# Queries and forget gates of six HGRN heads as seven block products, with their weight sums formed in the SSD

## The chip, the core and the metric

One core of a Trainium2 chip runs the whole kernel. The metric is the device time of one execution in microseconds (us), as the median of several runs. The engines are named as in the profile: PE is TensorE, DVE VectorE, ACT ScalarE, POOL GpSimdE and SP SyncE.

## The reference

The model has two layers over 512 tokens of width 1024, in float32. Layer 0 mixes the tokens by a Mamba-2 SSD, layer 1 by an HGRN2; after each mixer come a layer norm, an MLP with squared ReLU, another layer norm and a gated embedding. What matters here is the start of the HGRN: one projection to 4 x 1024 columns, of which the first two quarters are the queries `q` and the raw forget gates `fz`, split into 8 heads of 128 columns.

```python
q, f, v, g = split(u @ w_in, 4)         # u: 512 x 1024, w_in: 1024 x 4096; f is fz
log_f = logaddexp(log(lb), log1p(-lb) + log_sigmoid(fz))
k = (1 - lb) * sigmoid(-fz)
# per head, chunks of 64 tokens: a gated linear recurrence over q, k, v with decay f,
# then o = rms_norm(o) * silu(g), and o @ w_out
```

## The kernel before

**Products.** Each float32 operand is split into a high part `hi` (rounded to the fast float32 format fp32r) and the rest `lo`, and a product takes three matmuls, hi·hi, hi·lo and lo·hi: `mm3`, lines L120 to L122. For a weight, `unit` loads a tile of 128 x 1024 through SP's queue into a `raw` buffer, ScalarE casts it to `whi` (L114), and VectorE subtracts to get `wlo` (L116).

**Queries and gates.** `qf(h)` makes q and f of head h. Each is one PSUM bank `pj` of 128 x 512 (head columns by tokens): 8 steps over the model width, each an `mm3` with a 128 x 128 weight and 512 columns of tokens, so 24 matmuls for q and 24 for f. ScalarE copies q out of its bank (L1173), and makes f and k from the other one: two sigmoids (L1177, L1180) and two scalings (L1178, L1181). There are four `pj` banks in all.

**Block products.** `gated(i)`, which makes v and g of four heads at a time, uses a scheme with seven block products instead of eight (a Strassen-like one): the activations' sums `s1` to `s4` are formed in the HGRN's lead-in, and the weights' sums in the SSD, by `sums_early`, which loads four quarters on POOL's queue into one tile `b8`, adds and subtracts on VectorE (L437 and following), and stores the sums to device memory (`pre_h`), from where the HGRN reads them as ordinary weights. One PSUM bank there collects several products, and is read between them.

**Order of work.** TensorE's instructions run in the order in which the code writes them. On the other engines a scheduler puts them in order by its own estimate of when each can run. In the HGRN TensorE's work comes from two generators that are interleaved by hand. The foreground is `scores(n)` and `tail(n)` for pair n of heads: score matmuls (`blocks`, L1263 and L1371), which VectorE masks and multiplies into place (L1294, L1295, L1306, L1275), and a tail of transposes, value products (L1432, L1434), the norm (ScalarE's squares L1438 and square root L1441, VectorE's reciprocal L1443 and scaling L1447). The background is the list `JOBS`: `q0` to `q7` are the heads' `qf`, `b0` and `b1` the two `gated`, `o` the output projection. Between steps of the foreground `fill(amount)` takes background work worth that amount (a full-width `mm3` counts 0.68); the amounts are in `GAPS`, a row for each pair of heads.

In the SSD a loop over k = 1 to 8 makes two steps a round, and calls `next(sums)` up to three times in round 1 and twice in the others.

Of the kernel before, what the change touches and what calls it, by code (L numbers as in the profile page):

```python
# [32 lines left out]
SUMS = (60, 300, 300, 300)  # L33

JOBS = "q0 s0 q1 s1 q2 q3 b0 q4 q5 q6 q7 b1 o".split()
LEADIN = 6.0
GAPS = (6.0, 12.0, 10.0, 10.0), (13.0, 9.5, 9.5, 9.5), (10.0, 10.0, 10.0, 10.0), (14.0, 5.0, 4.0, 3.5), (3.0, 2.0, 2.5, 0.0)
CONSTS = dict(ident=P, triu=P, eps=1, convw=96, convb=24, dskip=16, snw=16, dtc=2, hlb=8, hnw=1)


# [1 line left out]
def trunk(ctx: ExitStack, tc, a):  # L42
# [21 lines left out]
    def mk(p, shape, tag, dt=F32, **kw):  # L64
        return p.tile(list(shape), dt, tag=tag, name=nm(tag), **kw)
# [34 lines left out]
    def behind(ins):  # L100
        return nullcontext() if ins is None else tc.issue_after(ins.ins)
# [323 lines left out]
    def sums_early(w, dst):  # L425

        for u in range(2):
            for h in range(2):
                cs = slice(h * 512, (h + 1) * 512)
                t = mk(b8, [P, 4, T], "b8")  # L430
                nc.gpsimd.tensor_copy(t[:, :, 0], toks[0][:, :, 0])
                w00, w01, w10, w11 = (t[:, i] for i in range(4))
                for x, src in zip((w01, w11, w00, w10), (w[0][1], w[1][1], w[0][0], w[1][0])):
                    nc.gpsimd.dma_start(x, src[u][:, cs])
                yield
                with behind(marks["pe"]):
                    nc.vector.tensor_sub(w11, w11, w01)  # L437
# [556 lines left out]

    whvg = a["whvg"]
    heads = [[[[whvg[8 * i + 4 * n + 2 * r + u] for u in range(2)] for n in range(2)] for r in range(2)] for i in range(2)]
    sums = (step for i in range(2) for step in sums_early(heads[i], a["pre_h"][i]))

    PIECES = {3: (0, 4), 4: (2, 2), 5: (0, 4), 6: (2, 2)}

    with tc.manual_schedule(engines={mybir.EngineType.PE}):
        bcm[0] = bc_group(0)
        for j in range(2):
            load_decay(j)
            x_part(j)
            z_part(j)
        prep[0] = bc_prep(bcm[0], bank(pst, "pt"), bank(psy, "py0"))
        toks.extend(dt_tail())
        turn_pair(0, (bank(psy, "py1"), bank(psj, "pj")))
        for k in range(1, 9):  # L1010
            i, j = 2 * k, 2 * k + 1
            mine, theirs = PIECES.get(k, (0, 0))
            with behind(conv[1][1] if k == 1 else None):
                decays(i - 2)
            if k < 8:
                if k in (4, 6):
                    bcm[k // 2] = bc_group(k // 2)
# [144 lines left out]
    def qf(h):  # L1162
# [18 lines left out]
        nc.scalar.activation(kk, kk, AF.Copy, scale=lbc[:, h : h + 1])  # L1181
# [22 lines left out]
    def background():  # L1204
        first = gated(0)
        for _ in range(8):
            yield next(first)
        for f in late:
            f()
        for job in JOBS:  # L1210
            i = int(job[1:] or 0)
            if job == "o":
                yield from out0()
            elif job[0] == "s":
                nc.gpsimd.dma_start(a["xd"][:, i], acc[:, i])
# [392 lines left out]
```

## Time and profile before

| | |
|---|---|
| median of 3 runs | 1392.22 us (1392.14 to 1393.08) |
| the profiled execution | 1393.39 us |
| its span (first to last instruction) | 1391.6 us |
| TensorE busy | 1385.1 us (100%) |
| VectorE / ScalarE / GpSimdE busy | 79% / 58% / 4% |
| SSD, about | 0 to 330 us |
| HGRN, about | 755 to 990 us |

All times inside the span are counted from its start. A row of the timeline gives start, duration, engine, line, operation, destination and sources, shape and count, and in brackets how long the engine stood idle before it and what released it. A row of a line's view gives the duration's minimum, median and maximum in ns. A row of a stretch gives, behind its length, the busy time and instruction count of PE, its weight loads, DVE, ACT and POOL, then the clock granted to TensorE, the share of the DMA engines and GB/s. `mean ns of one` for a matmul counts overlapped time; the pitch of its starts is what it costs.

### The profile page before, as it was taken

To read this page: it belongs to the slowest core of one execution; us is meant where nothing else is said; L and a number is where in the kernel's file an instruction comes from. 1 tells how busy PE (TensorE), PEld (TensorE's weight loads), DVE (VectorE), ACT (ScalarE), POOL (GpSimd) and SP (SyncE) were. 2 spreads that over 40 slices of the span, in tenths; PEclk is the share of its full clock that TensorE was granted. 3 is DMA by queue.
4 is the path that set the end of the run, shared out by engine and by line. 5 is a ranking of instruction groups with operands and counts; after the bars stand their busy time and mean duration, and the time that the engine had idled before them with its cause. 6 is when DMAs were issued, how large, how long until landed. Compare 5 with 4: busy or idle time off the path is not lost.

```text
span 1391.6 us, 20632 instructions
## 1 busy us (share of the span) xinstructions
PE 1385.1 (100%) x7885; PEld 1157.9 (83%) x7885; DVE 1104.6 (79%) x1734; ACT 811.7 (58%) x1309; POOL 50.4 (4%) x101
## 2 busy tenths in 40 slices
PE   9999999999999999999999999999999999999998
PEld 7888888888988888888888888888888888888887
DVE  7798976686867879778889886878785887769886
ACT  7877667485455455546466465674555554545563
POOL 0220200100000000000000000000000000000000
PEclk9999999999999999999999999999999999999999
DMA  8675533523354665654385343254263656646374
GB/s 290 220 254 171 212 137 130 188 97 101 114 206 151 213 221 171 209 186 165 106 305 195 124 145 99 93 178 143 97 221 128 205 185 216 219 151 210 107 247 148
DMA packets 74819, 241.96 MB, mean 174 GB/s; under 512 B 9056, under 2 KB 9696, under 8 KB 74592
## 3 DMA queue, kind: packets, MB, share of 16 engines
q1 hardware_dynamic: 57792, 197.64, 42.2%
q0 software_dynamic: 7712, 26.22, 5.3%
q10 hardware_dynamic: 9216, 16.78, 3.3%
q8 instruction: 62, 1.02, 0.3%
q14 instruction: 37, 0.30, 0.1%
HBM read 211.18 MB, written 29.43 MB: 173 GB/s over the span
## 4 chain that ended last, share of the span: by engine, by line
PE 92%; DVE 3%; ACT 2%; DMA 2%; issue 0%; POOL 0%; SPq 0%; DVEq 0%; ACTq 0%
PE pj L120 23%; PE pj L122 23%; PE pj L121 23%; PE py L120 5%; PE py L122 5%; PE py L121 5%; DMA raw<-in_wssd 1%; PE py L939 1%; PE py L1263 1%; DVE cv L811 1%; DVE wlo L116 1%; ACT b L906 1%; PE py L941 1%; DMA acc<-in_xw 0%; PE pt L922 0%
## 5 line engine op out<-in xcount | busy, mean ns | idle before, releaser
L114 ACT CAST whi<-raw 128x1024 fp32r<-128x1024 f32 x234 | 244.8, 1050 | 256.5 <-PE pj L121 125.0
L116 DVE TENSOR_TENSOR wlo<-raw,whi 128x1024 fp32r<-128x1024 f32 x234 | 284.8, 1222 | 131.3 <-ACT whi L114 129.9
L120 PE MATMUL pj<-b,whi 128*128 128x512 f32 (+1 forms) x992 | 377.9, 382 | 0.0
L121 PE MATMUL pj<-b,whi 128*128 128x512 f32 (+1 forms) x992 | 375.8, 379 | 0.0
L122 PE MATMUL pj<-b,wlo 128*128 128x512 f32 (+1 forms) x992 | 375.8, 379 | 0.0
L122 PEld LDWEIGHTS pj<-b,wlo 128*128 128x128 f32 x992 | 186.5, 188 | 35.1
L121 PEld LDWEIGHTS pj<-b,whi 128*128 128x128 f32 x992 | 186.6, 188 | 34.6
L120 PEld LDWEIGHTS pj<-b,whi 128*128 128x128 f32 x992 | 186.1, 188 | 34.8
L122 PE MATMUL pj<-whi,b 128*128 128x512 f32 (+1 forms) x482 | 187.5, 389 | 0.0
L120 PE MATMUL pj<-whi,b 128*128 128x512 f32 x448 | 176.7, 395 | 0.0
L121 PE MATMUL pj<-wlo,b 128*128 128x512 f32 x448 | 174.4, 390 | 0.0
L114 ACT CAST whi<-r 128x1024 fp32r<-128x1024 f32 x64 | 67.2, 1053 | 89.6 <-PE pj L121 67.7
L122 PEld LDWEIGHTS pj<-whi,b 128*128 128x128 f32 x482 | 90.5, 188 | 18.8 <-DVE b L1458 0.2
L120 PE MATMUL py<-whi,b 128*128 128x512 f32 x256 | 100.4, 392 | 0.0
L122 PE MATMUL py<-whi,b 128*128 128x512 f32 x256 | 99.7, 389 | 0.0
L121 PE MATMUL py<-wlo,b 128*128 128x512 f32 x256 | 99.6, 389 | 0.0
L116 DVE TENSOR_TENSOR wlo<-r,whi 128x1024 fp32r<-128x1024 f32 x64 | 77.8, 1220 | 27.4 <-ACT whi L114 26.8
L120 PEld LDWEIGHTS pj<-whi,b 128*128 128x128 f32 x448 | 84.1, 188 | 17.4 <-ACT b L1457 0.3
L121 PEld LDWEIGHTS pj<-wlo,b 128*128 128x128 f32 x448 | 84.2, 188 | 16.9
L120 PEld LDWEIGHTS py<-whi,b 128*128 128x128 f32 x256 | 48.1, 188 | 10.2 <-DVE acc L489 0.5
L122 PEld LDWEIGHTS py<-whi,b 128*128 128x128 f32 x256 | 48.0, 188 | 10.1
L121 PEld LDWEIGHTS py<-wlo,b 128*128 128x128 f32 x256 | 48.1, 188 | 9.8
(421 smaller groups left out, 2083.8 us busy)
## 6 DMA issues: line engine op xcount, KB each, us to landing
raw<-in_w SPq DMA_DIRECT2D x112, 512.0 KB, 3.8
r<-in_w SPq DMA_DIRECT2D x64, 512.0 KB, 4.0
raw<-in_wssd SPq DMA_DIRECT2D x38, 512.0 KB, 4.7
a<-csd SPq DMA_DIRECT2D x16, 512.0 KB, 4.1
b<-in_whvg POOLq DMA_DIRECT2D x32, 256.0 KB, 5.4
pre_h<-b POOLq DMA_DIRECT2D x32, 256.0 KB, 3.0
raw<-in_wso SPq DMA_DIRECT2D x16, 512.0 KB, 4.1
pre<-sg ACTq DMA_DIRECT2D x32, 256.0 KB, 4.7
```

Of the source, the lines that this page charges most:

```text
L114: nc.scalar.copy(hi[:, :n], f)
L116: nc.vector.tensor_sub(lo[:, :n], f, f32(hi[:, :n]))
L120: nc.tensor.matmul(out, sh, mh, start=start, stop=False, **kw)
L121: nc.tensor.matmul(out, sh, ml, start=False, stop=False, **kw)
L122: marks["pe"] = nc.tensor.matmul(out, sl, mh, start=False, stop=stop, **kw)
L811: got = nc.vector.scalar_tensor_tensor(cv[:, d:], ps[:, : T - d], convw[:, i, k : k + 1], cv[:, d:], ALU.mult, ALU.add)
L906: nc.scalar.activation(m[:, r, sl], csb[:, r, sl], AF.Relu, scale=-1.0, bias=cs_tok[:, c, 2 * j + r : 2 * j + r + 1])
L939: nc.tensor.matmul(yd[64 * r : 64 * r + 64, sl], xdt[:, c, r, :], m[:, r, sl], start=True, stop=c == 0)
L941: nc.tensor.matmul(yd[64 * r : 64 * r + 64, sl], pv[:, c - 1, r, :], ecs[:, r, (c - 1) * P : c * P], start=False, stop=True,)
L1263: nc.tensor.matmul(ps[r][32 * b : 32 * b + 32, base + n * c : base + n * c + n], kk[r][:, ts], moving(r, 4 * c + b), start=True, stop=True,)
```

## The change

For heads 2 to 7 `qf` is replaced by `qf_blocks`. The four blocks of the product are q and f by two halves of the tokens, and the model width is split in two as well; seven products of 128 x 256, each of four `mm3` steps, take the place of eight. Two banks `px` and `py` hold them: x collects four products one after the other and is read after each; y holds two, z (the other half of `py`) one. The parts that were copied or added out lie in half of a tile `pre`. ScalarE copies after P1, P2 and P3 (L1226, L1229, L1231), VectorE adds after P4, P5 and P6 (L1234, L1236, L1238); after P7 the gates are made (L1241 to L1251), the sigmoids in two halves each. `sums_head` forms the weights' sums, one tile of four loads, four operations and four stores a head. A tile of `sums_early` is now finished in one step instead of two; the first step of round 1 falls away. `GAPS` of pair 3 gets smaller amounts.

```diff
+BLOCKED = (2, 3, 4, 5, 6, 7)
+SUM_STEPS = (1, 1)
-GAPS = ..., (14.0, 5.0, 4.0, 3.5), (3.0, 2.0, 2.5, 0.0)
+GAPS = ..., (9.5, 5.0, 3.7, 3.4), (3.0, 2.0, 2.5, 0.0)
...
                     for n, x in ((2, w11), (0, w01)):
                         nc.gpsimd.dma_start(dst[n, u][:, cs], x)
-                yield
-                with behind(marks["pe"]):
                     nc.vector.tensor_add(w00, w11, w00)
                     nc.vector.tensor_sub(w10, w10, w00)
...
+    def sums_head(w, dst):
+
+        t = mk(b8, [P, 4, T], "b8")
+        nc.gpsimd.tensor_copy(t[:, :, 0], toks[0][:, :, 0])
+        b11, b12, b21, b22 = (t[:, i] for i in range(4))
+        for x, src in zip((b12, b22, b11, b21), (w[1][:, :T], w[1][:, T:], w[0][:, :T], w[0][:, T:])):
+            nc.gpsimd.dma_start(x, src)
+        yield
+        with behind(marks["pe"]):
+            nc.vector.tensor_sub(b22, b22, b12)
+            nc.vector.tensor_sub(b12, b12, b11)
+            ...
+            nc.vector.tensor_add(b11, b22, b11)
+            nc.vector.tensor_sub(b21, b21, b11)
+            ...
-    sums = (step for i in range(2) for step in sums_early(heads[i], a["pre_h"][i]))
+    wholes = [sums_early(heads[i], a["pre_h"][i]) for i in range(2)]
+    wholes[1:1] = [sums_head([a["whq"][2 * h + w] for w in range(2)], a["pre_q"][h]) for h in BLOCKED]
+    sums = (step for whole in wholes for step in whole)
...
             states(k - 1)
-            if k == 1:
-                next(sums)
             decays(i - 1)
...
-            next(sums)
+            if (k, 0) >= SUM_STEPS:
+                next(sums, None)
...
-            next(sums, None)
+            if (k, 1) >= SUM_STEPS:
+                next(sums, None)
...
+    def qf_blocks(h):
+        ...
+        px, py = bank(psj, "pj"), bank(psj, "pj")
+        x, y, z = px[:, 0:256], py[:, 0:256], py[:, 256:512]
+        ...
+        def product(w, at, moving, ps, start):
+            hi, lo = w
+            for k in range(4):
+                c = slice((4 * at + k) * P, (4 * at + k + 1) * P)
+                mm3(ps, hi[:, c], lo[:, c], moving[0](k), moving[1](k), start and k == 0, k == 3, skip_group_check=True)
+                yield 0.36
+        ...
+        raw = unit(a["whq"][2 * h])
+        yield from product(raw, 0, part(0, 0), x, True)
+        nc.scalar.copy(q1, x)
+        t32 = unit(a["pre_q"][h][0])
+        yield from product(t32, 0, block(mix["s3"]), y, True)
+        nc.scalar.copy(fz, y)
+        yield from product(t32, 1, block(mix["s2"]), x, False)
+        nc.scalar.copy(q2, x)
+        t41 = unit(a["pre_q"][h][1])
+        yield from product(t41, 0, part(1, 1), y, False)
+        vec.tensor_add(q2, y, q2)
+        yield from product(t41, 1, block(mix["s1"]), x, False)
+        vec.tensor_add(fz, x, fz)
+        yield from product(raw, 1, part(1, 0), z, True)
+        vec.tensor_add(q1, z, q1)
+        yield from product(unit(a["whq"][2 * h + 1][:, T:]), 0, block(mix["s4"]), x, False)
+        ...
+        nc.scalar.activation(f[:, 0:256], x, AF.Sigmoid)
+        nc.scalar.activation(f[:, 256:512], fz, AF.Sigmoid)
+        ...
-                yield from qf(i)
+                yield from (qf_blocks if i in BLOCKED else qf)(i)
```

The new lines push the numbers of all later ones: `mm3` is L122 to L124, the cast L116, the subtraction L118, and what was L1263 to L1456 in `scores` and `tail` is 70 higher.

What moves where, at three places. First ScalarE while head 2's products run. Ahead of these rows stand the sigmoids of head 1 (`f_6759` and `f_6843` are its f; `qt` is a tile of `scores` for the first pair). Before:

```order
L1180 ACTIVATE k_6762<-pj_6734 128x512
L1178 ACTIVATE f_6759<-f_6759,lb_6566,lbc_6568 128x512 [waits Activation_49]
L1181 ACTIVATE k_6762<-k_6762,lbc_6568 128x512 [waits Activation_49]
L1317 COPY qt_6972<-qo_6862 128x32x4 [waits DVE_49]
L114 CAST whi_7143<-raw_7141 128x1024 [waits DMAHW3_49,PE_49]
L1173 COPY qx_6812<-pj_6777 128x32x16 [waits PE_49]
L114 CAST whi_7149<-raw_7147 128x1024 [waits DMAHW4_49,PE_49]
L1177 ACTIVATE f_6915<-pj_6820 128x512 [waits DVE_49,PE_49]
```

The same place in the changed kernel, where `b_1141_6855` is the tile `pre`, and `pj_6856` and `pj_6857` are `px` and `py` of head 2:

```order
L1200 ACTIVATE k_6846<-pj_6818 128x512
L1198 ACTIVATE f_6843<-f_6843,lb_6650,lbc_6652 128x512 [waits Activation_49]
L1201 ACTIVATE k_6846<-k_6846,lbc_6652 128x512 [waits Activation_49]
L1226 COPY b_1141_6855<-pj_6856 128x256 [waits PE_49]
L1229 COPY b_1141_6855<-pj_6857 128x256 [waits PE_49]
L1387 COPY qt_7133<-qo_6979 128x32x4 [waits DVE_49]
L116 CAST whi_7177<-raw_7175 128x1024 [waits DMAHW3_49,PE_49]
L1231 COPY b_1141_6855<-pj_6856 128x256 [waits PE_49]
L116 CAST whi_7222<-raw_7220 128x512 [waits DMAHW4_49,PE_49]
```

The copies of P1, P2 and P3 (L1226, L1229, L1231) stand in this queue behind head 1's last gates; the third one also stands behind the `qt` copy and a cast.

Second VectorE during head 2, where the score matmuls of the first pair's first step come (`py_1148` and `py_1149` are their banks before, `py_1157` and `py_1158` now). Before:

```order
L116 TENSOR_TENSOR wlo_7145<-raw_7141,whi_7143 128x1024 [waits DMAHW3_49,PE_49,Activation_49]
L1294 TENSOR_TENSOR k_6691<-k_6691,gg_6869 128x128x2 [waits PE_49]
L1295 TENSOR_TENSOR k_6691<-k_6691,f_6688 128x128
L1306 TENSOR_TENSOR scd_6783<-py_1148_6827,mf_6550 128x8x4x4
L1325 TENSOR_TENSOR gg_6976<-tot_6863 128x32 [waits DVE_49]
L1294 TENSOR_TENSOR k_6762<-k_6762,gg_6879 128x128x2 [waits PE_49]
L1295 TENSOR_TENSOR k_6762<-k_6762,f_6759 128x128
L1275 COPY_PREDICATED scd_6783<-mu_6552,py_1148_6827 128x8x3x4 [waits DVE_49]
L1306 TENSOR_TENSOR scd_6784<-py_1149_6828,mf_6550 128x8x4x4
L1275 COPY_PREDICATED scd_6783<-mu_6552,py_1148_6827 128x8x2x4 [waits DVE_49]
L1275 COPY_PREDICATED scd_6784<-mu_6552,py_1149_6828 128x8x3x4 [waits DVE_49]
L1275 COPY_PREDICATED scd_6783<-mu_6552,py_1148_6827 128x32 [waits DVE_49]
```

In the changed kernel:

```order
L1365 TENSOR_TENSOR k_6775<-k_6775,f_6772 128x128
L1376 TENSOR_TENSOR scd_6869<-py_1157_6944,mf_6634 128x8x4x4
L1395 TENSOR_TENSOR gg_7137<-tot_6980 128x32 [waits DVE_49]
L1364 TENSOR_TENSOR k_6846<-k_6846,gg_6996 128x128x2 [waits PE_49]
L1365 TENSOR_TENSOR k_6846<-k_6846,f_6843 128x128
L1345 COPY_PREDICATED scd_6869<-mu_6636,py_1157_6944 128x8x3x4 [waits DVE_49]
L1376 TENSOR_TENSOR scd_6870<-py_1158_6945,mf_6634 128x8x4x4
L1345 COPY_PREDICATED scd_6869<-mu_6636,py_1157_6944 128x8x2x4 [waits DVE_49]
L1345 COPY_PREDICATED scd_6870<-mu_6636,py_1158_6945 128x8x3x4 [waits DVE_49]
L1345 COPY_PREDICATED scd_6869<-mu_6636,py_1157_6944 128x32 [waits DVE_49]
L1345 COPY_PREDICATED scd_6870<-mu_6636,py_1158_6945 128x8x2x4 [waits DVE_49]
L1236 TENSOR_TENSOR b_1141_6855<-pj_6856,b_1141_6855 128x256 [waits PE_49]
```

The addition of P5 (L1236) stands at the end of the score instructions, of which L1364, L1376 and L1345 were L1294, L1306 and L1275.

Third VectorE during head 5, around the output block of the first pair's tail. In the kernel before, at the tail of the second pair, the same instructions with what followed them there:

```order
L1349 TENSOR_TENSOR xc_8350<-qt_8166,tot_8015 128x4x2x32 [waits DVE_49]
L1353 COPY_PREDICATED scd_7950<-mu_6552,py_1321_8131 128x4x16
L1350 TENSOR_TENSOR xc_8350<-xc_8350,tot_8015 128x4x32 [waits DVE_49]
L1443 RECIPROCAL hri_8307<-hms_8297 128x8 [waits Activation_49]
L1353 COPY_PREDICATED scd_7951<-mu_6552,py_1322_8132 128x4x16
L1447 SCALAR_TENSOR_TENSOR qo_8281<-pt_8279,hri_8307,b_6575 128x128 [waits DVE_49]
L1447 SCALAR_TENSOR_TENSOR qo_8281<-pt_8279,hri_8307,b_6575 128x128 x3
L1447 SCALAR_TENSOR_TENSOR qo_8282<-pm_8280,hri_8307,b_6575 128x128 x4
L116 TENSOR_TENSOR wlo_8540<-raw_8536,whi_8538 128x1024 [waits DMAHW5_49,Activation_49]
```

In the changed kernel, where `pj_7909` and `pj_7908` are head 5's `py` and `px`:

```order
L1423 COPY_PREDICATED scd_7550<-mu_6636,py_1269_7784 128x4x16
L1420 TENSOR_TENSOR xc_8031<-xc_8031,tot_7615 128x4x32 [waits DVE_49]
L1513 RECIPROCAL hri_7988<-hms_7978 128x8 [waits Activation_49]
L1423 COPY_PREDICATED scd_7551<-mu_6636,py_1270_7785 128x4x16
L1517 SCALAR_TENSOR_TENSOR qo_7962<-pt_7960,hri_7988,b_6658 128x128 [waits DVE_49]
L1517 SCALAR_TENSOR_TENSOR qo_7962<-pt_7960,hri_7988,b_6658 128x128 x3
L1517 SCALAR_TENSOR_TENSOR qo_7963<-pm_7961,hri_7988,b_6658 128x128 x4
L1234 TENSOR_TENSOR b_1141_6855<-pj_7909,b_1141_6855 128x256 [waits PE_49]
L1236 TENSOR_TENSOR b_1141_6855<-pj_7908,b_1141_6855 128x256 [waits PE_49]
L118 TENSOR_TENSOR wlo_8298<-raw_8294,whi_8296 128x512 [waits DMAHW4_49,Activation_49]
L1238 TENSOR_TENSOR b_1141_6855<-pj_7909,b_1141_6855 128x256 [waits PE_49]
```

The additions of P4 and P5 (L1234, L1236) stand behind the reciprocal and the eight scalings (L1517); on TensorE, the matmuls of that output block stand between P3 and P4.

More of the change, by code (lines that the diff above doesn't have):

```diff
@@ L35 @@
 JOBS = "q0 s0 q1 s1 q2 q3 b0 q4 q5 q6 q7 b1 o".split()
+BLOCKED = (2, 3, 4, 5, 6, 7)
+SUM_STEPS = (1, 1)
 LEADIN = 6.0
-GAPS = (6.0, 12.0, 10.0, 10.0), (13.0, 9.5, 9.5, 9.5), (10.0, 10.0, 10.0, 10.0), (14.0, 5.0, 4.0, 3.5), (3.0, 2.0, 2.5, 0.0)
+GAPS = (6.0, 12.0, 10.0, 10.0), (13.0, 9.5, 9.5, 9.5), (10.0, 10.0, 10.0, 10.0), (9.5, 5.0, 3.7, 3.4), (3.0, 2.0, 2.5, 0.0)
 CONSTS = dict(ident=P, triu=P, eps=1, convw=96, convb=24, dskip=16, snw=16, dtc=2, hlb=8, hnw=1)
@@ L446, in sums_early @@
                         nc.gpsimd.dma_start(dst[n, u][:, cs], x)
+    def sums_head(w, dst):
[8 more added lines that the diff above has]
+            nc.vector.tensor_sub(b12, b12, b11)
+            for to, x in ((dst[0][:, :T], b22), (dst[1][:, T:], b12)):
+                nc.gpsimd.dma_start(to, x)
+            nc.vector.tensor_add(b11, b22, b11)
+            nc.vector.tensor_sub(b21, b21, b11)
+            for to, x in ((dst[0][:, T:], b11), (dst[1][:, :T], b21)):
+                nc.gpsimd.dma_start(to, x)
     def ready(dst, n):
@@ L1182, in qf @@
         made["q", h] = q, f, kk
+    def qf_blocks(h):
+        if "pre" not in mix:
+            mix["pre"] = mk(b8, [P, 2, D], "b8")
+        px, py = bank(psj, "pj"), bank(psj, "pj")
+        x, y, z = px[:, 0:256], py[:, 0:256], py[:, 256:512]
+        part = lambda r, n: tuple(
+            lambda k, f=f: f(4 * r + k, slice(256 * n, 256 * n + 256)) for f in (x_s.h, x_s.l)
+        )
+        block = lambda t: tuple(lambda k, u=u: t[:, u, k, :] for u in range(2))
+        def product(w, at, moving, ps, start):
[4 more added lines that the diff above has]
+                yield 0.36
+        qs = mix["pre"][:, h % 2, 0:512]
+        q1, q2, fz = (mix["pre"][:, h % 2, 256 * n : 256 * n + 256] for n in range(3))
+        raw = unit(a["whq"][2 * h])
[14 more added lines that the diff above has]
+        yield from product(unit(a["whq"][2 * h + 1][:, T:]), 0, block(mix["s4"]), x, False)
+        q = tmp("qx", [P, 32, 40])
+        nc.scalar.copy(
+            q[:, :, 0:16].rearrange("p n (r j) -> p n r j", r=4), qs.rearrange("p (n j r) -> p n r j", n=32, r=4)
+        )
+        f = tmp("f", [P, T])
+        nc.scalar.activation(f[:, 0:256], x, AF.Sigmoid)
+        nc.scalar.activation(f[:, 256:512], fz, AF.Sigmoid)
+        nc.scalar.activation(f, f, AF.Identity, scale=lbc[:, h : h + 1], bias=lb[:, h : h + 1])
+        kk = tmp("k", [P, T])
+        nc.scalar.activation(kk[:, 0:256], x, AF.Sigmoid, scale=-1.0)
+        nc.scalar.activation(kk[:, 256:512], fz, AF.Sigmoid, scale=-1.0)
+        nc.scalar.activation(kk, kk, AF.Copy, scale=lbc[:, h : h + 1])
+        made["q", h] = q, f, kk
@@ L1600 @@
     args["pre_h"] = nc.dram_tensor("pre_h", (2, 4, 2, P, D), F32).ap()
+    args["pre_q"] = nc.dram_tensor("pre_q", (8, 2, P, D), F32).ap()
     args["xd"] = nc.dram_tensor("xd", (P, NCH, D), F32).ap()
```

## The prediction

> **What bounds the kernel now.** I read the head of the page first: how busy each engine is, the granted clock, and the chain of work that ended last.
>
> ```profile
> span 1391.6 us, 20632 instructions
> PE 1385.1 (100%) x7885; PEld 1157.9 (83%) x7885; DVE 1104.6 (79%) x1734; ACT 811.7 (58%) x1309; POOL 50.4 (4%) x101
> PEclk9999999999999999999999999999999999999999
> PE 92%; DVE 3%; ACT 2%; DMA 2%; issue 0%; POOL 0%; SPq 0%; DVEq 0%; ACTq 0%
> ```
>
> TensorE is busy all the time, at its full clock, and carries 92% of the chain. Next I asked what TensorE waits for; these three rows are the whole answer of the view of waits.
>
> ```profile
> PE pm L155 <- DVE y L152: 1.1, 1, 1.1
> PE py L120 <- ACT whi L174: 0.7, 1, 0.7
> PE py L972 <- DVE ss L967: 0.5, 1, 0.5
> ```
>
> 2.3 us in all, none of it in the HGRN. So the time is the length of TensorE's stream of instructions, and a change can act in two ways only: it shortens that stream, or it opens a hole in it. Third, the timeline of TensorE, for the pitch (start to start) of the two shapes in question, since the durations of pipelined matmuls overlap.
>
> ```profile
> 344.79 0.39 PE L121 MATMUL pj<-wlo,b 128*128 128x512 f32 x1
> ...
> 357.26 0.40 PE L122 MATMUL pj<-whi,b 128*128 128x512 f32 x1
> ...
> 367.47 0.28 PE L120 MATMUL pj<-b,whi 128*128 128x256 f32 x1
> ...
> 370.22 0.28 PE L122 MATMUL pj<-b,wlo 128*128 128x256 f32 x1
> ```
>
> 55 intervals lie between the first two rows: 12.47 / 55 = 0.2267 us for 512 columns. 23 lie between the last two: 2.75 / 23 = 0.1196 us for 256. Half the columns cost 53%.
>
> **Part 1: the matmuls.** A head's q and f were 2 x 8 steps of three matmuls, 48 x 0.2267 = 10.88 us. They become 7 products of 12 matmuls, 84 x 0.1196 = 10.05 us. That is 0.83 us a head, and for heads 2 to 7 a gain of 4.98 us, all on the bound.
>
> A reason against this would be the weight loads, of which there are now 84 instead of 48 a head:
>
> ```profile
> L122 PEld LDWEIGHTS pj<-b,wlo 128*128 128x128 f32 x992 | 186.5, 188 | 35.1
> ```
>
> The 256-column row above has a load for each matmul, and its pitch (0.120) is shorter than one load (0.188): the loads overlap and the pitch already holds them. The Trainium skill says otherwise ("TensorE: Matmul & The Clock Gate", The mechanism and LDWEIGHTS): a load of 128 columns takes 107 ns and overlaps with matmuls only where the row groups differ. By it a 256-column matmul would take about 0.107 + 0.107 = 0.213 us and a 512-column one 0.320, a head 17.9 us instead of 15.4, and the six heads would lose some 15 us; the trace disagrees at both shapes (0.120 and 0.227).
>
> **Part 2: work added beside TensorE.** Unit prices:
>
> ```profile
> L114 ACT CAST whi<-raw x234: 1030/1053/1082, 14.8 to 1369.8; 128x1024 fp32r<-128x1024 f32 x117
> L116 DVE TENSOR_TENSOR wlo<-raw,whi x234: 1192/1222/1364, 15.8 to 1371.1; 128x1024 fp32r<-128x1024 f32 x117
> L1139 ACT ACTIVATE b<-pj x8: 375/383/400, 833.7 to 940.5; 128x256 f32<-128x256 f32 x8
> L1132 DVE TENSOR_TENSOR b<-pj,b x8: 407/413/438, 819.9 to 929.3; 128x256 f32<-128x256 f32 x8
> L437 DVE TENSOR_TENSOR b<-b x8: 681/692/694, 50.8 to 253.5; 128x512 f32<-128x512 f32 x8
> ```
>
> In the HGRN a head casts 3.5 weight tiles instead of 2, copies three products out on ScalarE and adds three on VectorE. ScalarE: 1.5 x 1.05 + 3 x 0.38 + about 0.4 for gates cut in halves = 3.1 us. VectorE: 1.5 x 1.22 + 3 x 0.41 = 3.1 us. Six heads: 18.5 us on each. The loads on SyncE's queue grow from 1.0 to 1.75 MB a head. In the SSD, each head adds one tile of sums: 4 loads and 4 stores on GpSimdE's queue, 4 x 0.69 us on VectorE, 16.6 us for six. The room for this:
>
> ```profile
> 55.00:110.00 55.00, 55.00 (x341) 46.38 (x340) 53.49 (x79) 46.41 (x81) 12.29 (x22) 1.00 0.70 235
> 790.00:838.00 48.00, 48.00 (x469) 39.22 (x468) 40.93 (x120) 30.40 (x57) 0.00 (x0) 1.00 0.40 133
> 890.00:941.00 51.00, 51.00 (x506) 42.96 (x505) 39.12 (x103) 34.58 (x80) 2.38 (x5) 1.00 0.47 156
> ```
>
> The columns after TensorE and its loads are VectorE, ScalarE, GpSimdE, clock, DMA share, GB/s. The HGRN has some 15 to 23% of VectorE free, a third of ScalarE, half of the DMA. 18.5 us spread over the 200 us from 780 bring VectorE from about 80 to about 90%: it fits as an average, so as throughput I cost it at nothing. In the SSD the tight place is 55 to 110 us, with VectorE 1.5 us from full. But the heads' sums come in only after the first four whole tiles, as the order of `wholes` in the code has it, at and past that stretch; as many sums as before stand in it. I take 0 there, with 0 to 2.5 us as bounds (four 0.69 us sums falling into it would be 2.8, less a little of the 1.5). Nothing is under zero: no step of the SSD on TensorE got shorter.
>
> **Part 3: the turnarounds, where I put the cost.** A product of 12 matmuls lasts 12 x 0.1196 = 1.44 us, and the seven products P1 to P7 share two PSUM banks in turn. So P3 waits for ScalarE's copy of P1, P4 for that of P2, P5 for that of P3, P6 for VectorE's addition of P4, P7 for that of P5. In the head before, a bank was filled for 5.4 us and four banks went round. Now each copy or addition has one product, 1.44 us, and needs about 0.4 of it; engines work in order, so it is late as soon as more than 1.0 us of other work stands ahead of it. What stands ahead is in the orders shown above; how long it takes is in the trace. Head 2 in rows of before (ScalarE, then TensorE and VectorE):
>
> ```profile
> 780.43 1.05 ACT L114 CAST whi<-raw 128x1024 fp32r<-128x1024 f32 x1 [3.42 <-PE pj L121]
> 781.88 0.59 ACT L1180 ACTIVATE k<-pj 128x512 f32<-128x512 f32 x1
> 783.06 0.72 ACT L1181 ACTIVATE k<-k,lbc 128x512 f32<-128x512 f32 x1
> 786.12 0.30 ACT L1317 COPY qt<-qo 128x128 f32<-128x128 f32 x1 [2.34 <-DVE qo L1288]
> 786.32 1.05 ACT L114 CAST whi<-raw 128x1024 fp32r<-128x1024 f32 x1
> ```
>
> ```profile
> 780.46 0.39 PE L120 MATMUL pj<-b,whi 128*128 128x512 f32 x1
> ...
> 787.35 1.31 PE L1263 MATMUL py<-qx,k 128*32 128x80 f32 x64
> 788.59 0.50 PE L120 MATMUL pj<-b,whi 128*128 128x512 f32 x1
> ```
>
> ```profile
> 788.46 1.22 DVE L116 TENSOR_TENSOR wlo<-raw,whi 128x1024 fp32r<-128x1024 f32 x1
> 789.60 0.42 DVE L1294 TENSOR_TENSOR k<-k,gg 128x256 f32<-128x256 f32 x1
> ...
> 792.88 0.34 DVE L1326 TENSOR_TENSOR gg<-tot,gg 128x32 f32<-128x32 f32 x1
> ```
>
> - P1 runs 780.46 to 781.90. P2 needs a bank that the k sigmoid of head 1 frees at 781.88 + 0.59 = 782.47: stall 0.57.
> - P2 ends 783.91. The copy of P1 stands behind head 1's last gate, 783.06 + 0.72 = 783.78, and ends 784.16: P3 stalls 0.25.
> - P3 ends 785.60, P4 787.04. The copy of P3 stands behind the qt copy, which VectorE's L1288 holds until 786.12, and the cast behind it: 787.37 + 0.38 = 787.75. P5 stalls 0.71.
> - After half of P5 come the 64 score matmuls (787.35 to 788.59, 1.24 us), then the rest of P5 and P6, which ends 791.87. P7 needs the addition of P5. Ahead of that, VectorE has the twelve instructions (L1294 to L1275) that wait for those score matmuls: 792.88 - 789.60 = 3.28 us. They start about 0.3 us after the score matmuls, at 790.0, so the addition ends 790.0 + 3.28 + 0.42 = 793.7. P7 stalls 1.85.
>
> Head 2 loses 3.4 us. Head 5 meets the output block of a tail (lines L1432 to L1447); a row of each engine, from the second pair's block:
>
> ```profile
> 907.13 0.60 PE L1432 MATMUL pt<-a,sc 128*128 128x128 f32 x4
> 911.01 0.50 PE L120 MATMUL pj<-whi,b 128*128 128x512 f32 x1
> ```
>
> ```profile
> 911.61 1.28 ACT L1441 ACT_TABLE_LOAD   x1
> ```
>
> ```profile
> 913.43 0.19 DVE L1443 RECIPROCAL hri<-hms 128x8 f32<-128x8 f32 x1
> 914.70 1.12 DVE L1447 SCALAR_TENSOR_TENSOR qo<-pm,hri,b 128x128 f32<-128x128 f32 x4
> ```
>
> In the new order this block stands right before P4, and VectorE's addition of P4 behind the reciprocal (which waits for ScalarE's table load and square root) and all eight L1447. P6 could start 911.01 - 907.13 + 2 x 1.44 = 6.8 us after the block's start; the addition ends (914.70 + 1.12 - 907.13) + 0.33 = 9.0. P6 stalls 2.3 us.
>
> The other late places I count the same way, from the rows above. Head 4, P6: ten score instructions, at the 0.27 us each that 3.28 / 12 gives, 0.3 us and an addition, 3.3, against 2.5 us of matmuls: 0.7. Head 7, P6: seventeen of them, 5.3 us, against three products: 1.0, and its P5 0.3. Head 6: copies of scores stand ahead of its copies, 0.65; heads 3 and 5, gates ahead of theirs, 0.15 and 0.45. These six terms make 3.3 us and are estimates. Bounds of the whole: at least 2.0 (half of the two large single waits), if VectorE runs ahead in the holes made earlier; at most 15, if each of the 36 turnarounds in the six heads is late by the 0.4 us of its own instruction.
>
> **Sum.** -5.0 (matmuls) + 3.4 + 2.3 + 3.3 (turnarounds) + 0 (SSD) = +4.0 us. The profiled execution took 1393.39 us, 1.8 more than its span and 1.2 more than the median of the runs, 1392.22; the difference of 4 us is carried over to the median: 1396.3 us.
>
> **Rivals.** (a) Faster: the turnarounds hide, and only the count of matmuls is left, 1392.2 - 5.0 = 1387.2 us. For it: VectorE, not full, may work off its queue in any hole. It decides where all stalls together stay under 2.2 us (5.0 less 0.2% of the time, 2.8 us). Against it: L1294 and the reciprocal wait for TensorE's own work, so VectorE cannot have done them earlier. (b) Stalls of 2.2 to 7.8 us, so much smaller that they cancel the gain: about 1392.5 us. For it: my smaller terms rest on a few tenths each. (c) VectorE becomes the bound: 90% on average, with its casts' second halves late for the products that need them. If one such 1.22 us subtraction a head comes late on top, 7.3 us more, 1403. (d) The load rule above, by a row's nearest form: if loads of 0.188 us did not overlap, a head would lose 36 x 0.188 - 0.83 = 5.9 us; the 0.120 pitch excludes it. The skill's rule that independent groups of matmuls should rotate through PSUM banks, so that the emptying of one overlaps the next ("Perfetto Trace Analysis", Matmuls), speaks for my forecast: two banks and 1.44 us are little rotation; that TensorE of before shows no wait with four banks and 5.4 us agrees.
>
> **Numbers.** 0.2% of the time is 2.8 us, about what a measurement of this kernel can tell from no change: 1389.4 to 1395.0. Forecast (stalls 7.8 to 14 us) 0.53; (b) 0.27; (a) 0.14; (c), with (d), 0.06. Faster 0.14, same 0.27, slower 0.59. The range 1390 to 1402 leaves out most of (a) and (c), some 0.19. The forecast's own range is 1395 to 1401.
>
> **What would show it.** The view of waits gains rows of TensorE on ScalarE's copies and VectorE's additions of the products, together 7 to 11 us, the longest near 2 us at head 2's P7 and head 5's P6. The 256-column pitch stays 0.120. VectorE reads near 90% from 790 to 975. No new waits in the first 330 us. If those rows sum to under 2 us, part 3 is wrong; if TensorE waits in the SSD, part 2 is.

## The result and the profile after

| | before | changed |
|---|---|---|
| median | 1392.33 us (5 runs) | 1406.72 us (5 runs, 1406.52 to 1413.13) |
| ratio | | 1.0117 (95%: 1.0104 to 1.0130) |
| span of the profiled execution | 1391.6 us | 1404.9 us |

The changed kernel is 14.4 us slower, 1.2%: slower, as forecast, but by more than three times the 4 us forecast and outside the range of 1390 to 1402. First the head of the page of the changed kernel and three stretches of it (length, then busy time of PE, of its loads, of DVE, ACT and POOL, the granted clock, the DMA share and GB/s); behind them the view of waits of TensorE (who waits, on whom, us in all, how often, the longest).

```profile
span 1404.9 us, 21318 instructions
PE 1387.7 (99%) x8101; PEld 1168.1 (83%) x8101; DVE 1135.7 (81%) x1788; ACT 840.5 (60%) x1358; POOL 78.7 (6%) x155
...
165.00:220.00 55.00, 52.01 (x274) 42.78 (x274) 41.99 (x59) 30.68 (x49) 14.15 (x27) 0.97 0.64 216
840.00:890.00 50.00, 45.95 (x533) 42.65 (x523) 37.71 (x104) 34.67 (x78) 0.00 (x0) 0.97 0.39 128
790.00:975.00 185.00, 177.18 (x1991) 156.38 (x1990) 158.86 (x427) 124.70 (x267) 3.31 (x7) 0.99 0.48 158
```

```profile
PE pt L940 <- DVE xdt L908: 2.9, 1, 2.9
PE pj L122 <- DVE b L1234: 2.9, 3, 2.1
PE pj L122 <- ACT b L1231: 2.0, 3, 1.2
PE pj L122 <- DVE b L1236: 1.5, 1, 1.5
PE pm L157 <- DVE y L154: 1.1, 1, 1.1
PE pj L122 <- ACT b L1226: 1.0, 2, 0.8
PE pj L122 <- ACT k L1200: 0.5, 1, 0.5
```

TensorE, which in the middle of the program had waited once, for 0.5 us (L972 above), now has holes at two places: one in the SSD (L940 waits for VectorE's L908) and a series in the HGRN, on the copies L1226 and L1231 and the additions L1234 and L1236. In two stretches the granted clock is 0.97, where it was 1.00.

Where the 13.3 us of span come from can be read from instructions that both programs have, by their starts in the timeline of TensorE. Near the SSD's end, before and after:

```profile
284.46 0.59 PE L922 MATMUL pm<-xw,btok 128*128 128x256 f32 x2
```

```profile
288.50 0.67 PE L940 MATMUL pm<-xw,btok 128*128 128x256 f32 x2
```

And behind the HGRN, at the first transposes of its output:

```profile
1013.45 0.41 PE L224 MATMUL pt<-cst,acc 128*128 128x128 f32 x2
```

```profile
1026.90 0.30 PE L226 MATMUL pt<-cst,acc 128*128 128x128 f32 x1 [0.29 <-DVE acc L217]
```

4.0 us are lost near the end of the SSD, 13.45 - 4.04 = 9.4 us from there to the end of the HGRN, and nothing more behind it.

**The hole in the SSD.** TensorE, VectorE and GpSimdE of the changed kernel:

```profile
192.97 0.39 PE L124 MATMUL pj<-b,wlo 128*128 128x512 f32 x1
196.25 1.10 PE L940 MATMUL pt<-xw,btok 128*128 128x256 f32 x4 [2.90 <-DVE xdt L908]
...
199.15 0.63 PE L124 MATMUL pj<-b,wlo 128*128 128x512 f32 x1
199.58 0.63 PE L122 MATMUL pj<-b,whi 128*128 128x512 f32 x1
```

```profile
176.85 0.69 DVE L457 TENSOR_TENSOR b<-b 128x512 f32<-128x512 f32 x1 [1.78 <-DMA b<-in_whq]
179.58 0.69 DVE L458 TENSOR_TENSOR b<-b 128x512 f32<-128x512 f32 x1 [2.03 <-DMA b<-in_whq]
184.29 0.69 DVE L457 TENSOR_TENSOR b<-b 128x512 f32<-128x512 f32 x1 [4.02 <-DMA b<-in_whq]
```

```profile
171.31 0.19 POOL L451 COPY b<-toks 128x4 f32<-128x4 f32 x1 [2.11 <-DMA pre_q<-b]
171.96 2.21 POOL L454 DMA_DIRECT2D b<-in_whq  x4 [0.46 <-POOL b L451]
...
175.53 2.19 POOL L454 DMA_DIRECT2D b<-in_whq  x4 [0.41 <-POOL b L451]
```

The two steps of round 5 come close together. Their loads were issued at 172 and 175.5, and VectorE stood in its queue before them for 7.8 us, with work behind it that TensorE needs: L908 came late, and TensorE had a hole of 2.9 us. Why the loads came late is in the first row of GpSimdE: it takes the buffer of a tile (L451) only when the stores of an earlier tile have landed, and the loads then took 5.7 us in the median, while VectorE stood before them already at 175.1. Behind the hole the 512-column pitch is 0.43 us instead of 0.2267 (199.15 to 199.58): half the clock, as the stretch shows (the column behind GpSimdE's):

```profile
197.60:201.01 3.41, 3.41 (x9) 2.66 (x10) 3.41 (x6) 3.41 (x11) 0.93 (x2) 0.50 1.02 303
```

**The largest hole in the HGRN**, head 5's P6:

```profile
874.28 0.28 PE L124 MATMUL pj<-acc,wlo 128*128 128x256 f32 x1
876.62 0.41 PE L122 MATMUL pj<-b,whi 128*128 128x256 f32 x1 [2.05 <-DVE b L1234]
...
879.59 0.41 PE L124 MATMUL pj<-acc,wlo 128*128 128x256 f32 x1
879.81 0.41 PE L122 MATMUL pj<-acc,whi 128*128 128x256 f32 x1
```

```profile
873.83 0.20 DVE L1513 RECIPROCAL hri<-hms 128x8 f32<-128x8 f32 x1
...
875.11 1.12 DVE L1517 SCALAR_TENSOR_TENSOR qo<-pm,hri,b 128x128 f32<-128x128 f32 x4
876.15 0.42 DVE L1234 TENSOR_TENSOR b<-pj,b 128x256 f32<-128x256 f32 x1
```

The addition of P4 stands behind the reciprocal and the eight scalings. After this hole, too, the clock is halved: 0.21 us a matmul instead of 0.12, until about 880.2; the 17 slow intervals cost 1.6 us more than at full clock. The 3.41 us before, with the hole in them, and the 3.41 us behind:

```profile
873.44:876.85 3.41, 1.36 (x12) 1.15 (x11) 3.41 (x16) 3.17 (x11) 0.00 (x0) 1.00 0.03 8
876.85:880.26 3.41, 3.41 (x18) 3.41 (x18) 1.06 (x3) 1.99 (x3) 0.00 (x0) 0.50 0.41 154
```

### The profile page after: what moved, and what is told of

Same layout as the page of the kernel before. It is cut to its first block, busy times and chain, and to the rows that moved or that the text cites. A ratio compares the mean times of both kernels' runs of the same rounds, so it can differ in the third digit from the quotient of the medians.

```text
span 1404.9 us, 21318 instructions
## 1 busy us (share of the span) xinstructions
PE 1387.7 (99%) x8101; PEld 1168.1 (83%) x8101; DVE 1135.7 (81%) x1788; ACT 840.5 (60%) x1358; POOL 78.7 (6%) x155
## 4 chain that ended last, share of the span: by engine, by line
PE 80%; DVE 8%; ACT 6%; DMA 3%; issue 2%; POOL 0%; DVEq 0%; ACTq 0%; POOLq 0%; SPq 0%
PE pj L122 19%; PE pj L123 19%; PE pj L124 19%; PE py L122 5%; PE py L124 5%; PE py L123 5%; DVE wlo L118 2%; ACT whi L116 1%; DMA raw<-in_wssd 1%; DMA b<-in_whq 1%; ACT b L924 1%; PE py L957 1%; DVE scd L1345 1%; DVE cv L829 0%; DMA raw<-pre_q 0%
## 5 line engine op out<-in xcount | busy, mean ns | idle before, releaser
L116 ACT CAST whi<-raw 128x1024 fp32r<-128x1024 f32 x246 | 255.0, 1040 | 235.9 <-PE pj L123 113.2
L122 PE MATMUL pj<-b,whi 128*128 128x512 f32 (+1 forms) x1016 | 376.2, 371 | 4.4 <-DVE b L1234 2.9
L118 DVE TENSOR_TENSOR wlo<-raw,whi 128x1024 fp32r<-128x1024 f32 x246 | 295.6, 1208 | 103.8 <-ACT whi L116 102.0
L124 PE MATMUL pj<-b,wlo 128*128 128x512 f32 (+1 forms) x1016 | 373.2, 368 | 0.0
L122 PEld LDWEIGHTS pj<-b,whi 128*128 128x128 f32 x1016 | 191.8, 189 | 37.5 <-DVE b L1234 3.7
L124 PEld LDWEIGHTS pj<-b,wlo 128*128 128x128 f32 x1016 | 192.3, 189 | 31.4
L123 PEld LDWEIGHTS pj<-b,whi 128*128 128x128 f32 x1016 | 192.3, 189 | 31.2
L124 PE MATMUL pj<-whi,b 128*128 128x512 f32 (+1 forms) x482 | 187.6, 390 | 0.0
L122 PE MATMUL pj<-whi,b 128*128 128x512 f32 x448 | 177.1, 396 | 0.2 <-DVE b L1238 0.2
L116 ACT CAST whi<-r 128x1024 fp32r<-128x1024 f32 x64 | 67.2, 1053 | 89.9 <-PE pj L123 70.3
L124 PEld LDWEIGHTS pj<-whi,b 128*128 128x128 f32 x482 | 90.5, 188 | 18.8 <-DVE b L1528 0.2
L122 PE MATMUL py<-whi,b 128*128 128x512 f32 x256 | 100.3, 392 | 0.0
L118 DVE TENSOR_TENSOR wlo<-r,whi 128x1024 fp32r<-128x1024 f32 x64 | 77.8, 1221 | 27.2 <-ACT whi L116 25.9
L124 PE MATMUL py<-whi,b 128*128 128x512 f32 x256 | 99.7, 389 | 0.0
L122 PEld LDWEIGHTS pj<-whi,b 128*128 128x128 f32 x448 | 84.1, 188 | 18.0 <-DVE b L1238 0.5
L122 PEld LDWEIGHTS py<-whi,b 128*128 128x128 f32 x256 | 48.1, 188 | 10.2 <-DVE acc L507 0.5
L124 PEld LDWEIGHTS py<-whi,b 128*128 128x128 f32 x256 | 48.1, 188 | 10.1
```

Of the source, the lines that this page charges most:

```text
L116: nc.scalar.copy(hi[:, :n], f)
L118: nc.vector.tensor_sub(lo[:, :n], f, f32(hi[:, :n]))
L122: nc.tensor.matmul(out, sh, mh, start=start, stop=False, **kw)
L123: nc.tensor.matmul(out, sh, ml, start=False, stop=False, **kw)
L124: marks["pe"] = nc.tensor.matmul(out, sl, mh, start=False, stop=stop, **kw)
```

## The experiments

**The SSD's part.** Sums alone, first: all heads as `qf`.

```diff
-                yield from (qf_blocks if i in BLOCKED else qf)(i)
+                yield from qf(i)
-... (9.5, 5.0, 3.7, 3.4) ...
+... (14.0, 5.0, 4.0, 3.5) ...
```

> Sums of the six heads are formed in the SSD as in the changed kernel, but all heads use the whole-width products of before and the old amounts in GAPS. Theory: the part of the loss that shows before the HGRN is all the sums' doing: VectorE stands in its queue before late loads of the sums' tiles, TensorE gets the hole of about 3 us before L940 and a slow clock behind it, so +4.0 us, 1396.3 us (1395.3 to 1397.3). Rival, as my prediction had it: the sums are hidden and the 4 us come with the rest of the change, 1392.3 us.

1401.9 us (1400.1 to 1404.2), ratio 1.0071 (1.0054 to 1.0088). More than expected: the sums alone cost 9 us, by far not nothing, and unlike the kernel before they vary from run to run by 4 us. TensorE's row of waits:

```profile
PE pt L940 <- DVE xdt L908: 3.8, 1, 3.8
```

Then two halves of it. The traffic without VectorE's work:

```diff
-            nc.vector.tensor_sub(b22, b22, b12)
-            nc.vector.tensor_sub(b12, b12, b11)
...
-            nc.vector.tensor_add(b11, b22, b11)
-            nc.vector.tensor_sub(b21, b21, b11)
```

> The sums-alone kernel of the run before (1401.9 us, all heads at whole width), with the 24 additions and subtractions of the heads' sums left out: the tiles are loaded and stored as they are, so the traffic and the queue of GpSimdE stay and VectorE has nothing to wait for. Theory (VectorE stands in its queue before late loads): the loss of 7 to 9 us goes, 1392.0 to 1394 us, and TensorE has no wait on L908. Rival (the traffic delays other loads): at least half of the loss stays, 1396 us or more, with waits on casts of the SSD's weights.

1393.2 us, ratio 1.0011 (1.0001 to 1.0021); no wait on L908. The 48 transfers themselves cost some tenths of a per cent at most by the median; two of the ten runs took 1397.8 and 1398.6 us, which stays unexplained. And VectorE's work without the loads:

```diff
-        for x, src in zip((b12, b22, b11, b21), ...):
-            nc.gpsimd.dma_start(x, src)
+        h = [f32(x_s.h(i)) for i in range(4)]
...
-            nc.vector.tensor_sub(b22, b22, b12)
+            nc.vector.tensor_sub(b22, h[0], h[1])
```

> The sums-alone kernel (1401.9 us) with VectorE's 24 operations kept, but on data that lie in SBUF already: the 24 loads are left out, the stores stay (values of the sums differ; no head uses them). Theory (VectorE is held by late loads): 1392.5 to 1394.5 us, no hole before L940. Rival (VectorE has no time for 16.6 us more, wherever the loads are): half or more of the loss stays, 1396.5 us or more.

1400.2 us, ratio 1.0054 (1.0041 to 1.0068): by the time alone the rival wins. The trace says where:

```profile
282.44 0.39 PE L124 MATMUL pj<-b,wlo 128*128 128x512 f32 x1
287.15 0.76 PE L939 MATMUL pt<-xw,btok 128*128 128x256 f32 x1 [4.33 <-DVE xdt L907]
```

```profile
270.53 0.69 DVE L439 TENSOR_TENSOR b<-b 128x512 f32<-128x512 f32 x1 [4.68 <-DMA b<-in_whvg]
...
279.46 0.69 DVE L444 TENSOR_TENSOR b<-b 128x512 f32<-128x512 f32 x1 [1.65 <-DMA b<-in_whvg]
```

The hole in round 5, where the heads' loads were taken away, is gone; the same hole stands in round 7, where the tiles of v and g, pushed later by the heads' tiles, still have loads, and VectorE waits for those (7.6 us in four waits). So here, too, it stands before loads; my expectation that the time would come down was wrong, since I had looked at the heads' loads alone. Yet a wait for a load does not always cost. In the run with the traffic alone VectorE waited for the same tiles in round 7, and TensorE had no hole:

```profile
268.62 0.69 DVE L439 TENSOR_TENSOR b<-b 128x512 f32<-128x512 f32 x1 [1.46 <-DMA b<-in_whvg]
...
272.02 0.69 DVE L440 TENSOR_TENSOR b<-b 128x512 f32<-128x512 f32 x1 [2.11 <-DMA b<-in_whvg]
```

With the work, VectorE came 5.0 us later to what follows (281.21 for L974, against 276.23 for the same instruction, L971 there). No run keeps all the work and takes away every load, so that it is the waiting and not the work is read from the traces; no run shows it by itself.

Steps placed otherwise:

```diff
-SUM_STEPS = (1, 1)
+SUM_STEPS = (1, 0)
+SKIP = (5, 1), (6, 0)
...
+            if k == 1:
+                next(sums)
-            if (k, 0) >= SUM_STEPS:
+            if (k, 0) >= SUM_STEPS and (k, 0) not in SKIP:
```

> The changed kernel with the steps of the sums placed otherwise: three in round 1 as before, none at the second step of round 5 and the first of round 6, where the changed kernel's VectorE stood 7.8 us before loads. Theory: the hole before L940 and the slow clock behind it go: 1406.7 - 4 = 1402.7 us (1402 to 1403.7). Rival: the loads are late wherever the steps stand, because four of a tile wait for the stores of an earlier one; a hole opens at another place, 1405 us or more.

1404.1 us (1403.6 to 1408.3), ratio 1.0088. The 2.9 us wait before L940 fell to 0.5, but with fourteen tiles in fifteen steps other places got holes of 1.3 and 1.0 us (L991 at 111 us, and the first matmul of a product, which waits for VectorE's L830, at 212): between theory and rival. Last, the operations on GpSimdE:

```diff
-            nc.vector.tensor_sub(b22, b22, b12)
+            nc.gpsimd.tensor_sub(b22, b22, b12)
... (all four)
```

> The sums-alone kernel with the 24 operations on GpSimdE instead of VectorE. Theory as for the run without them: VectorE is never held by a load, 1392.0 to 1394.5 us. Rival 1 (traffic): 1396 us or more. Rival 2: GpSimdE's operations take so long that its own queue, which also issues the loads and stores of v and g, falls behind, and VectorE waits for those tiles: a new wait on L439, 1394.5 us or more.

1399.1 us, ratio 1.0039 (1.0021 to 1.0057). The time is that of the first rival, but the traffic alone had cost 0.6 us, and the second did not show: VectorE did not wait for the heads' tiles, it got slower. VectorE's L985 without and with GpSimdE at work, and what GpSimdE did then:

```profile
104.16 0.68 DVE L985 TENSOR_TENSOR ss<-ss,sq 128x512 f32<-128x512 f32 x1
...
112.07 1.75 DVE L985 TENSOR_TENSOR ss<-ss,sq 128x512 f32<-128x512 f32 x1
```

```profile
110.09 1.51 POOL L461 TENSOR_TENSOR b<-b 128x512 f32<-128x512 f32 x1
111.68 1.59 POOL L462 TENSOR_TENSOR b<-b 128x512 f32<-128x512 f32 x1
```

**The HGRN's part.** Block products alone: no sums for the heads, the second and third tile of a head from its own weights.

```diff
+        t32 = unit(a["whq"][2 * h + 1])
...
+        t41 = unit(a["whq"][2 * h])
```

> The block products of heads 2 to 7 alone: the heads' sums are not formed, and the second and third weight tile of a head are read from the head's own weights instead (the values differ, the shapes, loads and order do not); the sums of v and g are formed as before. Theory: what shows from the HGRN on is the block products' own doing, stalls of 8.5 us by the waits, slow clock behind the longest, less 5.0 us of matmuls, in all +9.4 to +10.4: 1401.7 to 1402.7 us. Rival: part of the HGRN's loss comes from the SSD's (buffers or loads late there): below 1400 us.

1400.4 us (1399.4 to 1400.7), ratio 1.0054 (1.0039 to 1.0069): +7.8 us, 2 less than I expected and between theory and rival. Between the two instructions used above (283.43 and 1021.04 here) its trace loses 8.6 us, against 9.4 in the changed kernel. In this trace the same holes stand as in the changed kernel, head 2's P7 and head 5's P6 with the same lengths, the slow clock behind the second again.

Next, the place in the queue: the six copies and additions with priority in the scheduler.

```diff
-        vec.tensor_add(q2, y, q2)
+        with tc.high_priority(offset=TURN):
+            vec.tensor_add(q2, y, q2)
... (all six)
```

> The changed kernel, with the three copies and three additions of a head given priority in the scheduler, so that on VectorE six instructions of the score block instead of twelve stand ahead of head 2's addition of P5, and head 5's addition of P4 stands ahead of the reciprocal. Theory (place in the queue): the hole at head 5's P6 (2.1 us) and the slow clock behind it go, and head 2's P7 loses about 1 us: 1406.7 - 5 = 1401.7 us (1400.5 to 1403.5), TensorE's wait on L1234 from 2.9 to under 1 us. Rival (VectorE full): what is pushed back is late instead, new waits on casts or scores take the place, 1405 to 1407.5 us.

1405.6 us, but from 1398.9 to 1412.2: the SSD's holes, which vary, cover it (this trace has two, 4.6 and 2.6 us). From the SSD's end to the HGRN's it loses 4.1 us against 9.4 in the changed kernel. The hole at head 5's P6 is gone and TensorE's wait on the additions of P4 is 0.3 us (L1238 here). A new one came where a copy fell behind a row of ScalarE's work:

```profile
PE pj L122 <- ACT b L1234: 2.4, 1, 2.4
...
PE pj L122 <- DVE b L1241: 0.4, 1, 0.4
...
PE pj L122 <- DVE b L1238: 0.3, 1, 0.3
```

So the theory holds for the two large holes, and shifting the order alone makes others. The other way is time: two heads in turn, heads 4 to 7 alone, no sums. In the changed kernel these four heads had 5.5 of the 7.9 us of waits.

```diff
+    def qf_pair(i):
+        two = [qf_blocks(i), qf_blocks(i + 1)]
+        for n in range(14):
+            for _ in range(4):
+                yield next(two[n % 2])
...
-JOBS = "... q4 q5 q6 q7 b1 o".split()
+JOBS = "... q4 q6 b1 o".split()
```

> Block products for heads 4 to 7 alone, the products of two heads in turn (P1 of head 4, P1 of head 5, P2 of head 4 and so on), so that three products, 4.3 us, lie between a bank's last matmul and its next; no sums for the heads (second and third weight tile read from the head's own weights, the values differ). Theory (each turnaround had one product's time): the stalls on the copies and additions fall from 8.5 us to under 1.5, and four heads gain 4 x 0.83 = 3.3 us: 1392.6 - 3.3 + 1 = 1390.3 us (1389.3 to 1391.5). Rival (VectorE or ScalarE too full for the products' weights): waits on casts and subtractions instead, 1393 us or more.

1394.5 us, ratio 1.0013 (1.0003 to 1.0022), 4 us more than I expected. All waits on the heads' copies and additions but one are gone; that one is 2.9 us:

```profile
PE pj L121 <- ACT b L1208: 2.9, 1, 2.9
```

With priority for the copies and additions as well:

> The run with two heads in turn and without sums (1394.45 us), with priority for the copies and additions. There one hole of 2.9 us was left, at head 6's P3: the copy of P1 stood behind two casts and six copies of scores on ScalarE. Theory (place in the queue): the hole goes, 1392.6 - 3.3 + 1 = 1390.3 us (1389.3 to 1391.7). Rival: ScalarE has a burst of gates and casts there, whatever its order, and the casts pushed back stall TensorE instead: 1393 us or more.

1393.5 us, ratio 1.0007 (0.9998 to 1.0016), again 3 us more than I expected. The hole is gone, and no hole is over 0.9 us; small ones on v's and g's copies (1.2 us), on two additions (0.8) and before a transpose (0.4) sum to 2.4 us and eat most of the 3.3 that the matmuls of four heads save. VectorE:

```profile
790.00:975.00 185.00, 182.49 (x2000) 158.82 (x1998) 158.18 (x431) 123.95 (x274) 3.33 (x7) 1.00 0.44 149
```

It is as busy (158.2 of 185 us) as in the changed kernel (158.9), where these four heads alone waited 5.5 us on their copies and additions instead of 0.8. That speaks against full engines as the cause, and for the place in the queue together with the time between a product and the next use of its bank. No run has all six heads in turn.

**Versions meant to beat both.** Four heads in turn with the sums on GpSimdE:

> A version meant to beat both: heads 4 to 7 as block products of two heads in turn, sums for those four heads alone, formed on GpSimdE, none at the second step of round 5 and the first of round 6. If both theories hold, 1390.3 us (1389 to 1392.5). If the sums' traffic is what costs, 1394 us or more; if GpSimdE's queue falls behind, a wait in the first 330 us.

1404.2 us, ratio 1.0082: slower VectorE (holes of 2.5 and 1.7 us on L991 and L249) and the 2.9 us on ScalarE's copy together. Then with priority, and the four heads' sums on VectorE behind all those of v and g, which keep two steps a tile for their first half:

```diff
+                if halves:
+                    yield
...
-    wholes[1:1] = [...]
+    wholes += [...]
+SKIP = (5, 1), (6, 0)
...
+        next(sums, None)
+        some(1)
+        next(sums, None)
```

> A version meant to beat both: heads 4 to 7 as block products of two heads in turn, copies and additions with priority, and the sums of these four heads after all those of v and g, from round 7 on and behind the SSD's loop; the first four tiles of v and g in two steps each, as before. Theory: VectorE's order up to round 6 is that of before, so no hole in the first 240 us, and later it has room: as the run without sums, plus up to 1 us for the traffic, 1390.8 us (1389.5 to 1392.3). Rival: the late sums meet the last group's chain, a wait between 240 and 330 us, 1393.5 us or more.

1393.5 us, ratio 1.0007 (0.9999 to 1.0016), the same as without sums. No row of the SSD is left in its waits, and VectorE at the place of the first hole does what it did before:

```profile
178.15 1.23 DVE L119 TENSOR_TENSOR wlo<-raw,whi 128x1024 fp32r<-128x1024 f32 x1 [3.55 <-ACT whi L117]
183.58 1.23 DVE L119 TENSOR_TENSOR wlo<-raw,whi 128x1024 fp32r<-128x1024 f32 x1 [4.21 <-ACT whi L117]
184.72 0.74 DVE L979 SCALAR_TENSOR_TENSOR y<-xs,cst,py 128x512 f32<-128x512 f32 x1
```

The sums of four heads are hidden there. VectorE still stands 4.6 us before their loads (three waits between 264 and 321 us), but nothing that TensorE needs comes late behind them. What was left were copies of v and g behind an output block on ScalarE. The last version moves the amounts:

```diff
-GAPS = ..., (13.0, 9.5, 9.5, 9.5), (10.0, 10.0, 10.0, 10.0), (11.2, 5.0, 3.8, 3.4), ...
+GAPS = ..., (13.0, 9.5, 9.5, 7.9), (8.4, 10.0, 10.0, 10.0), (14.0, 5.0, 4.0, 3.5), ...
```

> The run with four heads in turn and late sums (1393.54 us), with the 3.2 of amounts in GAPS that its block products save taken from rows 1 and 2, where these products run, instead of from row 3, so that the products of v and g of heads 4 to 7 stand against the second pair's output block as in the kernel before. There a hole of 1.7 us and one of 0.8 opened, because two of those products' copies came behind that block's squares and square root on ScalarE. Theory: both holes go and nothing else moves, 1391.0 us (1390.3 to 1392.0), 0.1% under the kernel before. Rival: the foreground that comes earlier now meets the heads' products, holes of the same length at 880 to 900 us, 1393 us or more.

1391.8 us (1391.1 to 1392.4), ratio 0.9992 (0.9983 to 1.0001): the fastest of all, 1.1 us under the kernel before, which this measurement can just not tell from no change. The hole of 1.7 us fell to 0.5 and a new one of 1.2 (L1504 on VectorE's L1177) came.

## Why the prediction was right or wrong

**Part 1, the matmuls: no run contradicts it.** The 256-column pitch is 0.12 us in every trace outside the slow-clock stretches; the load rule was excluded rightly.

**Part 3, the turnarounds: right in mechanism and in their sum.** The sum was 9.0 us; the waits on the heads' copies, additions and on k's sigmoid read 2.9 + 2.0 + 1.5 + 1.0 + 0.5 = 7.9. Head 2: P2 0.5 for 0.57, P5 0.5 for 0.71, P7 1.5 for 1.85 (P3 nothing for 0.25). Head 5's P6: 2.1 for 2.3; head 4's P6: 0.6 for 0.7. The other small terms hit the sum by luck: head 7 waited 1.2 us at P5 for the 0.3 forecast and 0.2 at P6 for 1.0, head 5's P3 0.8 for 0.45, head 3 not at all. From start to start the holes are 0.1 to 0.3 us longer than the view of waits tells (874.28 to 876.62 is 2.34, of which 0.12 is the pitch and 2.05 the wait).

**What that part left out is what a hole costs beside its wait.** I priced a hole at its wait. The one of 2.05 us cost 1.6 us more, since TensorE ran at half its clock for 3.4 us behind it. And the matmul before a wait and the one behind it take longer than the pitch (0.28 us to the end of the one, 0.22 from the start of the other to the next). So the stretch with the HGRN lost 9.4 us net instead of the forecast's 4.0. Added up over all starts of TensorE: -5.0 us for the matmuls, 8.4 of idle time (the 7.9 and shorter waits), 2.9 around these waits, 1.5 of slow clock, and some 1.5 where products resume after other shapes or after gaps under 0.1 us, together 9.3.

**Part 2, the SSD at nothing: the step that failed.** It read VectorE's room as an average by stretch, and bounded the cost at 2.5 us by the throughput of one stretch (55 to 110). The stretch that lost had 38.1 of 55 us busy before, 17 us free:

```profile
165.00:220.00 55.00, 55.00 (x298) 46.03 (x297) 38.14 (x52) 32.15 (x51) 5.31 (x9) 1.00 0.44 155
```

The cost was not VectorE's time but its queue: additions stand before a load that is not there yet, and what TensorE needs stands behind. The prediction counted the loads and stores of the sums and said nothing of when they land. Alone this cost 7 to 12 us in the runs, 4.0 in the profiled execution of the changed kernel, slow clock included. The two parts alone, 9.3 and 7.8 us, add to 17.1 where the whole lost 14.4; the SSD's part differs from run to run, and why is open. The changed kernel's trace loses 13.4 us, 9.4 more than the 4.0 forecast; 4.0 of these are this part, and 5.4 are what part 3 left out.

**The rivals.** (c), VectorE as the bound, with 1403 us, came nearest in time and is wrong in cause: 158 of 185 us busy went with 0.8 us of waits on the additions when two heads go in turn with priority. (a) and (b) did not happen. The sign that I had named against part 2, "if TensorE waits in the SSD", is the one that showed.

## What to carry to other kernels

Where one engine is the bound and never waits, cost a change by the queues, not by busy shares: for each new instruction ask what it waits for, and what stands behind it that the bound engine needs; a load is due when its user's turn comes, not when there is room. A bank that is read out between products needs more time to its next use than the longest row of work that can stand ahead of the reader; one product's 1.44 us was too little here, and two independent chains in turn give three without other buffers. Price a hole of more than 2 us in TensorE's stream at its length plus, as a chance, some 1.6 us of slow clock: nine of the thirteen holes of 2.2 to 4.8 us in these traces (counted from start to start less the pitch) were followed by it.

## What the runs showed of the hardware

- **Half clock in steps of 3.41 us.** Each trace holds the times at which the granted clock changed. Leaving out the first and the last 20 us of each span, it stood at half nine times in the fourteen traces, eight times for 3.41 us and once for 6.83. Two such stretches of one trace begin a whole number of 3.413 us apart: 679.25 us, 199 of them, in the changed kernel; 706.56, 207 of them, in the run with priority alone; 774.83, 227 of them, in that with four heads in turn and the sums on GpSimdE. Cut into windows on this grid, the traces have ten windows in which TensorE was idle for 2.05 us or more; behind each of them the clock was halved for one window. They have 21 with 0.9 to 1.9 us, and behind none of them was it. So the same wait of 2.05 us at head 5's P6 halved the clock in the changed kernel, where it lay in one window, and not in the run with the steps placed otherwise, where 1.1 and 0.9 us fell into two. The Trainium skill ("TensorE: Matmul & The Clock Gate", What's actually happening) tells of a free-running window of some 3.4 us in which TensorE must be idle for the clock to halve. The free-running window and its length agree; that it must be idle throughout does not, since 2.05 of 3.41 us were enough.
- **VectorE beside GpSimdE.** A VectorE addition of 128x512 took 0.68 us alone and 1.75 while GpSimdE added (1.51 us). The Trainium skill ("SBUF — State Buffer", Who interferes with whom) says that a VectorE instruction with two SBUF inputs contends with a GpSimdE instruction that reads SBUF; the trace agrees. VectorE's operations on `cv`, which read one input from the PSUM tile `pj`, took 0.74 us on average between 100 and 240 us in the run with the operations on GpSimdE (L829) and in the one with the traffic alone (L825).
